# A decoder trunk on one core: the SBUF addresses of the split weights and of the differences of x are changed

## The chip, the core and the metric

The kernel runs on one core of a Trainium2 chip. The core has a matrix engine (TensorE, PE in the profile, with its weight loads shown apart as PEld), VectorE (DVE), ScalarE (ACT), GpSimd (POOL) and SyncE (SP), which issues transfers. The engines work on SBUF, a memory of 128 partitions; a tile has the same byte address in each of them, and "address" means that byte within a partition here. TensorE multiplies a stationary operand of 128 x 128 (loaded by LDWEIGHTS) with an operand that is streamed past it, and writes to PSUM.

The metric is the device time in microseconds. The kernel before takes 1767.03 us (median of 2 runs, 1766.98 to 1767.09).

## The reference

Two post-norm decoder layers on 512 tokens of width 1024, float32. Each layer is a SwiGLU feed-forward, a mixer and a second feed-forward, each followed by a LayerNorm.

```python
def swiglu_ffn(x, w_gu, w_down):
    a, u = jnp.split(x @ w_gu, 2, axis=-1)
    return (jax.nn.silu(a) * u) @ w_down

for l in range(DEPTH):
    x = layer_norm(DEEPNORM_ALPHA * x + 0.5 * swiglu_ffn(x, ffn1_w_gu[l], ffn1_w_down[l]),
                   ln1_g[l], ln1_b[l])
    x = layer_norm(DEEPNORM_ALPHA * x + hybrid_mixer(x, w_in[l], w_out[l], attn_sinks[l],
                                                     rope_cos, rope_sin, ret_cos, ret_sin),
                   ln2_g[l], ln2_b[l])
    x = layer_norm(DEEPNORM_ALPHA * x + 0.5 * swiglu_ffn(x, ffn2_w_gu[l], ffn2_w_down[l]),
                   ln3_g[l], ln3_b[l])
```

The hidden width of a feed-forward is 2816. The mixer projects x to attention and retention heads, computes both, and projects the result back.

## The kernel before

**Split products.** Every large product is made of three matmuls (`mm3`, L183 to L185). A float32 operand is split into a high part, rounded to the type fp32r by ScalarE (`split`, L168), and a low part, the rest, made by VectorE (L169). The three matmuls are high x high, high x low, low x high. In the rows of the profile L183, L184 and L185 follow each other, over and over.

**Units.** Weights come from HBM into one of two raw tiles (`raw`, `rawp`), and are split in pieces of 128 x 1024 elements, called units: a high tile `uh` and a low tile `ul`. The pool `unit` holds six of each (`UBUFS`), taken in turn; `Weights.pump` splits the next unit as soon as one of the six is given back. Everything that reads a unit after that is TensorE. In the gate and up projections and the mixer's projections by columns a unit is the stationary operand and x is streamed; in the down product and in the projections by tokens the unit is streamed, 512 columns at a time, and x or the hidden state is stationary.

**x and its differences.** x lies transposed in `xh` and `xl` (its high and low parts, 16,384 bytes each). For nine of the eleven column pairs of a feed-forward, gate and up are computed by a scheme of seven products instead of eight on blocks of half the contraction and half the tokens (`glu7`). Three products stream blocks of x itself, and four stream differences of its blocks, which `sums_of_x` writes once per feed-forward into the tiles `Th` and `Tl` (16,384 bytes each, four blocks). All these matmuls have 256 columns. The down product uses the same scheme on blocks of 256 x 512 x 10 chunks, with `xh` and `xl` as the room for the split hidden state, and 512 columns.

**Order.** Each engine runs its instructions in program order, which the code writes out by hand: products in sequence, splits of the next units between them.

**Addresses.** The pools are laid out in SBUF in the order in which they are made, each tile behind the one before: `base` (identity, `mhalf`, `xh`, `xl`, `Y`), `rawp`, `unit` (first the six `uh`, then the six `ul`), `small`, and then the pools of each stage, which take turns in the rest. Tiles of 4096 bytes follow each other without gaps, so all six `uh` have the same address modulo 256, and so have the chunks within a tile, whose steps are 512, 1024 and 2048 bytes. In the built program the starts are, modulo 256:

```
identity 128   mhalf 128   xh 160   xl 160   Y 160   raw 160
uh 160 (all six)   ul 160 (all six)
hT, S, R, Th, Tl, hr, tail units 96        mixer's q, k, pT, yah, yal, vr 32
```

Of the kernel before, what the change touches and what calls it, by code (L numbers as in the profile page):

```python
# [7 lines left out]
F32 = mybir.dt.float32  # L8
F32R = mybir.dt.float32r
# [9 lines left out]
P = 128  # L19
# [27 lines left out]
class Weights:  # L47


    def __init__(self, T, items):  # L50
        self.T, self.items = T, items
        self.emitted = self.taken = self.out = 0
        self.ready = []
        self.raws = {}
        self.last = {raw: i for i, (raw, _, _, _) in enumerate(items)}
# [44 lines left out]
class Trunk:  # L100
    def __init__(self, tc, ctx):
        self.tc, self.nc = tc, tc.nc
        self.n = 0
        self.now = 0
        self.pin = True
        self.tasks = []
        self.later = []
        self.pace = None
        self.halves = 2
        nc = self.nc  # L110
        self.base = ctx.enter_context(tc.tile_pool(name="base", bufs=1))
        self.rawp = ctx.enter_context(tc.tile_pool(name="rawp", bufs=2))
        self.unit = ctx.enter_context(tc.tile_pool(name="unit", bufs=UBUFS))
        self.small = ctx.enter_context(tc.tile_pool(name="small", bufs=3))
        self.psum = ctx.enter_context(tc.tile_pool(name="psum", bufs=8, space=PSUM))
        self.ident = self.base.tile([P, P], F32, name="ident")
        make_identity(nc, self.ident)
        self.mhalf = self.base.tile([P, 8], F32, name="mhalf")
        nc.vector.memset(self.mhalf, -0.5)
        self.xh = self.base.tile([P, KC, SEQ], F32R, name="xh")  # L120
        self.xl = self.base.tile([P, KC, SEQ], F32R, name="xl")
        self.Y = self.base.tile([P, NT, D], F32, name="Y")
# [37 lines left out]
    def units(self, pool=None, tag="u", bufs=None):  # L160
        pool = pool or self.unit
        kw = {} if bufs is None else {"bufs": bufs}
        hi = pool.tile([P, 1024], F32R, tag=tag + "h", name=self.nm("uh"), **kw)
        lo = pool.tile([P, 1024], F32R, tag=tag + "l", name=self.nm("ul"), **kw)
        return hi, lo

# [356 lines left out]
    def ffn(self, g_, b, out=None):  # L523
        nc, tc, W = self.nc, self.tc, self.W
        with ExitStack() as ctx:
# [3 lines left out]
            gp = self.gpool = gctx.enter_context(tc.tile_pool(name=self.nm("ffng"), bufs=1))  # L529
            hT = hpool.tile([P, NF, SEQ], F32, name=self.nm("hT"))  # L530
            H = KC // 2
            Th = gp.tile([P, 4, H, 256], F32R, name=self.nm("Th"))
            Tl = gp.tile([P, 4, H, 256], F32R, name=self.nm("Tl"))

            def sums_of_x():

# [136 lines left out]
            pool = self.fpool = ctx.enter_context(tc.tile_pool(name=self.nm("ffnd"), bufs=1))  # L673
# [80 lines left out]
            def take():  # L754
                u, h = W.get(), ahead.pop(0)
                ahead.append(next(split, None))
                return u, h
# [17 lines left out]
            for n, (banks, new, more) in enumerate((  # L775
# [12 lines left out]
                for g in range(GROUPS):  # L788
                    u, h = take()
# [398 lines left out]
```

## Time and profile before

| | |
|---|---|
| median of the runs | 1767.03 us |
| span of the profiled execution | 1765.1 us |
| instructions | 29166 |
| HBM read | 212.38 MB, 122 GB/s over the span |

The profiled execution is one run on the chip; its span is 1.9 us shorter than the median of the runs. Its page gives busy times by engine, a strip of 40 slices, and the chain of work that ended last: from the last instruction back to whatever released each step. Groups of instructions carry a count, a busy sum and a mean duration. For matmuls the duration includes the way through the array, during which the next one runs already, so it is not the interval at which they start; intervals are read from start times in the order of time. A weight load (PEld) runs beside the matmul before it.

### The profile page before, as it was taken

Reading aid. Unit: us, or ns where it says so; the run is one execution under the profiler, and the core shown is the slowest. Engines: PE = TensorE matmul, PEld = TensorE weight load, DVE = VectorE, ACT = ScalarE, POOL = GpSimd, SP = SyncE. Lnnn points to the kernel's source line nnn. Section 1 sums busy time; section 2 is a strip of 40 time slices with the busy share of each in tenths; the row PEclk is TensorE's granted clock in tenths of the full one; section 3 lists DMA queues with packets and bytes.
Section 4 is the critical chain, followed back from the end, with each engine's and each line's share of the span. In section 5 each row is a group of like instructions: output and inputs, shape, how many; then the busy total and the mean of one; then the engine's idle time right before and its main releaser. Section 6 shows DMA issues by size and latency. Waiting matters only on the chain.

```text
span 1765.1 us, 29166 instructions
## 1 busy us (share of the span) xinstructions
PE 1752.7 (99%) x11930; PEld 1600.5 (91%) x11930; DVE 1414.9 (80%) x1975; ACT 928.1 (53%) x1456; POOL 182.9 (10%) x152
## 2 busy tenths in 40 slices
PE   9999999999999999999999999999999999999998
PEld 9999988887789999998899999889877899999886
DVE  7888888856767888878888888888567587888887
ACT  5455556378712455555535555554795234555561
POOL 0000022111111000014000000311011110000131
PEclk9999999999999999999999999999999999999999
DMA  6234389422222243369423334982233122334891
GB/s 191 97 96 133 131 202 199 131 85 88 73 79 72 74 137 102 97 208 214 140 68 99 121 96 147 211 203 91 85 95 96 48 95 97 97 96 132 211 218 48
DMA packets 163765, 216.34 MB, mean 123 GB/s; under 512 B 5168, under 2 KB 116528, under 8 KB 163632
## 3 DMA queue, kind: packets, MB, share of 16 engines
q1 hardware_dynamic: 141872, 172.55, 30.5%
q0 software_dynamic: 21760, 41.95, 13.1%
q8 instruction: 93, 1.52, 0.3%
q14 instruction: 40, 0.33, 0.1%
HBM read 212.38 MB, written 2.10 MB: 122 GB/s over the span
## 4 chain that ended last, share of the span: by engine, by line
PE 90%; issue 6%; DMA 1%; DVE 1%; POOL 1%; ACT 0%; SPq 0%; POOLq 0%; DVEq 0%
PE ps L183 29%; PE ps L185 29%; PE ps L184 29%; PE ps L476 1%; DMA raw<-in_ffn_w_gu_dram 1%; POOL sw L959 1%; PE ps L1067 1%; PE ps L1015 0%; PE ps L1029 0%; PE ps L1063 0%; PE ps L1050 0%; DMA retS<-c_retS_dram 0%; ACT sw L957 0%; DVE ul L169 0%; PE ps L1007 0%
## 5 line engine op out<-in xcount | busy, mean ns | idle before, releaser
L183 PE MATMUL ps<-xh,uh 128*128 128x256 f32 (+1 forms) x1616 | 482.2, 298 | 0.0
L185 PE MATMUL ps<-xh,ul 128*128 128x256 f32 (+1 forms) x1616 | 479.3, 297 | 1.0 <-DVE ul L169 0.9
L184 PE MATMUL ps<-xl,uh 128*128 128x256 f32 (+1 forms) x1616 | 478.5, 296 | 0.3 <-DVE xl L169 0.3
L168 ACT CAST uh<-raw 128x1024 fp32r<-128x1024 f32 (+1 forms) x274 | 237.1, 886 | 245.6 <-PE ps L184 140.1
L169 DVE TENSOR_TENSOR ul<-raw,uh 128x1024 fp32r<-128x1024 f32 (+1 forms) x274 | 273.3, 1013 | 62.2 <-ACT uh L168 61.6
L183 PE MATMUL ps<-Th,uh 128*128 128x256 f32 x1152 | 319.1, 277 | 0.0
L184 PE MATMUL ps<-Tl,uh 128*128 128x256 f32 x1152 | 318.7, 277 | 0.0
L185 PE MATMUL ps<-Th,ul 128*128 128x256 f32 x1152 | 318.3, 276 | 0.0
L185 PEld LDWEIGHTS ps<-xh,ul 128*128 128x128 f32 x1616 | 307.9, 191 | 10.1 <-DVE ul L169 1.6
L183 PEld LDWEIGHTS ps<-xh,uh 128*128 128x128 f32 x1616 | 307.9, 191 | 9.7 <-issue 1.6
L184 PEld LDWEIGHTS ps<-xl,uh 128*128 128x128 f32 x1616 | 308.0, 191 | 7.9 <-DVE xl L169 0.5
L183 PE MATMUL ps<-uh,xh 128*128 128x512 f32 x720 | 283.4, 394 | 0.5 <-ACT xh L168 0.5
L185 PE MATMUL ps<-uh,xl 128*128 128x512 f32 x720 | 280.8, 390 | 0.0
L184 PE MATMUL ps<-ul,xh 128*128 128x512 f32 x720 | 280.3, 389 | 0.0
L168 ACT CAST uh<-S 128x1024 fp32r<-128x1024 f32 x144 | 151.1, 1049 | 149.0 <-PE ps L184 145.2
L169 DVE TENSOR_TENSOR ul<-S,uh 128x1024 fp32r<-128x1024 f32 x144 | 175.9, 1222 | 60.1 <-ACT uh L168 59.5
L184 PEld LDWEIGHTS ps<-Tl,uh 128*128 128x128 f32 x1152 | 216.7, 188 | 0.0
L183 PEld LDWEIGHTS ps<-Th,uh 128*128 128x128 f32 x1152 | 216.6, 188 | 0.0
L185 PEld LDWEIGHTS ps<-Th,ul 128*128 128x128 f32 x1152 | 216.4, 188 | 0.0
L389 POOL DMA_DIRECT2D R<-in_ffn_w_down_dram x80 | 97.1, 1217 | 1020.7 <-DVE ul L169 930.0
L169 DVE TENSOR_TENSOR ul<-R,uh 128x1024 fp32r<-128x1024 f32 x120 | 145.1, 1221 | 25.8 <-ACT uh L168 25.7
L183 PEld LDWEIGHTS ps<-uh,xh 128*128 128x128 f32 x720 | 135.2, 188 | 30.1 <-issue 1.6
(143 smaller groups left out, 2362.4 us busy)
## 6 DMA issues: line engine op xcount, KB each, us to landing
raw<-in_ffn_w_gu_dram SPq DMA_DIRECT2D x86, 1024.0 KB, 5.5
R<-in_ffn_w_down_dram POOLq DMA_DIRECT2D x80, 512.0 KB, 7.6
raw<-in_w_in_dram SPq DMA_DIRECT2D x18, 1024.0 KB, 5.2
R<-in_ffn_w_down_dram SPq DMA_DIRECT2D x16, 1024.0 KB, 6.3
raw<-in_ffn_w_down_dram SPq DMA_DIRECT2D x12, 1024.0 KB, 7.2
R<-in_ffn_w_down_dram SPq DMA_DIRECT2D x8, 512.0 KB, 4.3
raw<-in_w_in_dram SPq DMA_DIRECT2D x8, 512.0 KB, 6.1
raw<-in_w_out_dram SPq DMA_DIRECT2D x8, 512.0 KB, 6.4
```

Of the source, the lines that this page charges most:

```text
L168: a = self.nc.scalar.copy(hi, src)
L169: b = self.low = self.nc.vector.tensor_sub(lo, src, hi.bitcast(F32))
L183: keep(mm(out, ah, bh, start=start, stop=False, **kw))
L184: keep(mm(out, ah, bl, start=False, stop=False, **kw))
L185: keep(mm(out, al, bh, start=False, stop=stop, **kw))
L389: self.nc.gpsimd.dma_start(src, rows(i, j, g * 2, 2), accum_op=ALU.add))
L476: nc.tensor.transpose(b[:, c * P : (c + 1) * P], src[:, c * P : (c + 1) * P], self.ident)
L959: nc.gpsimd.tensor_mul(sw[:, :n], sw[:, :n], S)
L1067: ins = nc.tensor.matmul(ob[:, o0 : o0 + HD], ST[h][:, n, :], vr[:, n, p * P + h * HD : p * P + (h + 1) * HD], start=n == 0, stop=n == 0 o ...
```

## The change

No computation changes, and no instruction, transfer or wait is added, removed or moved: on each of the five engines the same instructions stand in the same order before and after. Tiles get other addresses.

- The high tiles of the pool `unit` get 1032 elements instead of 1024, of which the first 1024 are used, so each starts 32 bytes further on, modulo 256, than the one before.
- `mhalf` moves from the pool `base` to a pool `near` of its own between `rawp` and `unit`. What followed it in `base` starts 32 bytes earlier; `unit` starts where it did.
- `Th` and `Tl` get 8 elements more, and their contents start 4 elements (16 bytes) in, in the first feed-forward of each layer, and at 0 in the second.
- The rest of SBUF follows: what lies behind the units moves by 192 bytes.

```diff
+        self.near = ctx.enter_context(tc.tile_pool(name="near", bufs=1))
+        self.mhalf = self.near.tile([P, 8], F32, name="mhalf")
+        nc.vector.memset(self.mhalf, -0.5)
         self.unit = ctx.enter_context(tc.tile_pool(name="unit", bufs=UBUFS))
...
-        self.mhalf = self.base.tile([P, 8], F32, name="mhalf")
-        nc.vector.memset(self.mhalf, -0.5)
...
-        hi = pool.tile([P, 1024], F32R, tag=tag + "h", name=self.nm("uh"), **kw)
+        width = 1032 if pool is self.unit else 1024
+        hi = pool.tile([P, width], F32R, tag=tag + "h", name=self.nm("uh"), **kw)[:, :1024]
         lo = pool.tile([P, 1024], F32R, tag=tag + "l", name=self.nm("ul"), **kw)
...
-            Th = gp.tile([P, 4, H, 256], F32R, name=self.nm("Th"))
-            Tl = gp.tile([P, 4, H, 256], F32R, name=self.nm("Tl"))
+            self.ffns += 4
+            off = self.ffns % 8
+            Th, Tl = (gp.tile([P, 4 * H * 256 + 8], F32R, name=self.nm(n))[:, off : off + 4 * H * 256]
+                      .rearrange("p (i k t) -> p i k t", i=4, k=H) for n in ("Th", "Tl"))
```

The starts in the built program after the change, modulo 256:

```
identity 128   xh 128   xl 128   Y 128   raw 128   mhalf 128
uh 160, 192, 224, 0, 32, 64   ul 96 (all six)
Th 48, Tl 80 (first feed-forward of a layer)    Th 32, Tl 64 (second)
hT, S, R, hr, tail units 32        mixer's q, k, pT, yah, yal, vr 224
```

More of the change, by code (lines that the diff above doesn't have):

```diff
@@ L109, in __init__ @@
         self.halves = 2
+        self.ffns = 0
         nc = self.nc
```

## The prediction

> **What bounds the kernel now.** I read the page first: busy shares, the clock row and the chain that ended last.
>
> ```profile
> span 1765.1 us, 29166 instructions
> ...
> PE 1752.7 (99%) x11930; PEld 1600.5 (91%) x11930; DVE 1414.9 (80%) x1975; ACT 928.1 (53%) x1456; POOL 182.9 (10%) x152
> ...
> PEclk9999999999999999999999999999999999999999
> ...
> PE 90%; issue 6%; DMA 1%; DVE 1%; POOL 1%; ACT 0%; SPq 0%; POOLq 0%; DVEq 0%
> PE ps L183 29%; PE ps L185 29%; PE ps L184 29%; PE ps L476 1%; DMA raw<-in_ffn_w_gu_dram 1%; POOL sw L959 1%; PE ps L1067 1%; PE ps L1015 0%; PE ps L1029 0%; PE ps L1063 0%; PE ps L1050 0%; DMA retS<-c_retS_dram 0%; ACT sw L957 0%; DVE ul L169 0%; PE ps L1007 0%
> ```
>
> TensorE is busy for 99% of the span at a full granted clock, and the three lines of `mm3` are 87% of the chain. Next the waits of TensorE, all of them:
>
> ```profile
> PE ps L468 <- POOL ident masks.py:199: 1.4, 1, 1.4
> PE ps L185 <- DVE ul L169: 0.9, 2, 0.7
> PE ps L1029 <- DVE rr L1032: 0.8, 2, 0.4
> PE ps L183 <- ACT xh L168: 0.5, 2, 0.2
> PE ps L476 <- DMA Y<-in_x_dram: 0.3, 1, 0.3
> PE ps L184 <- DVE xl L169: 0.3, 1, 0.3
> ```
>
> They add up to 4.2 us of 1765.1. So the time is the number of matmuls times the interval at which TensorE starts them. Third, the groups of its lines by form; the counts are what I need from them (the means are modelled durations that overlap, not intervals):
>
> ```profile
> L183 PE MATMUL ps<-xh,uh 128*128 128x256 f32 x1408 | 398.5, 283 | 0.0
> ...
> L183 PE MATMUL ps<-Th,uh 128*128 128x256 f32 x1152 | 319.1, 277 | 0.0
> ...
> L183 PE MATMUL ps<-uh,xh 128*128 128x512 f32 x720 | 283.4, 394 | 0.5 <-ACT xh L168 0.5
> ...
> L183 PE MATMUL ps<-xh,uh 128*128 128x512 f32 x208 | 83.6, 402 | 0.0
> ...
> L183 PE MATMUL ps<-b,yah 128*128 128x512 f32 x64 | 25.3, 396 | 0.0
> L183 PE MATMUL ps<-uh,hr 128*128 128x512 f32 x64 | 25.2, 394 | 0.0
> ...
> L183 PE MATMUL ps<-uh,uh 128*128 128x512 f32 x32 | 12.5, 389 | 0.0
> ```
>
> Each has a twin of equal count at L184 and L185, so 256-column matmuls that stream x: 3 x 1408 = 4224; 256-column ones that stream a difference of x: 3 x 1152 = 3456; 512-column ones with a unit from the pool of six: 3 x (720 + 208 + 32) = 2880; 512-column ones without such a unit: 3 x 128 = 384.
>
> Last the intervals, from the order of time inside a feed-forward. Start times are in us, rounded to 10 ns, so I count over many rows:
>
> ```profile
> 74.16 0.29 PE L183 MATMUL ps<-Th,uh 128*128 128x256 f32 x1
> ...
> 74.52 0.28 PE L183 MATMUL ps<-Th,uh 128*128 128x256 f32 x1
> 74.63 0.28 PE L184 MATMUL ps<-Tl,uh 128*128 128x256 f32 x1
> ...
> 76.78 0.28 PE L185 MATMUL ps<-Th,ul 128*128 128x256 f32 x1
> 76.90 0.28 PE L183 MATMUL ps<-xh,uh 128*128 128x256 f32 x1
> ...
> 78.08 0.28 PE L184 MATMUL ps<-xl,uh 128*128 128x256 f32 x1
> ...
> 79.52 0.28 PE L184 MATMUL ps<-xl,uh 128*128 128x256 f32 x1
> ```
>
> From 74.63 to 76.78 are 19 intervals: 113.2 ns each, streaming a difference. From 78.08 to 79.52 are 12: 120.0 ns each, streaming x. Same shape, same weights' pool, same clock, 6.8 ns apart. The switch is not sharp: the first ten after 76.90 take 1.18 us (118 ns), the first three after 74.16 take 0.36 us (120 ns). Beside them stands what runs at the same time:
>
> ```profile
> 78.32 0.28 PE L183 MATMUL ps<-xh,uh 128*128 128x256 f32 x1
> 78.32 0.19 PEld L184 LDWEIGHTS ps<-xl,uh 128*128 128x128 f32 x1
> ```
>
> The load of the next matmul's weights starts with the stream of this one. Both read SBUF. In the program before, x starts at byte 160 modulo 256, every unit at 160, a difference at 96. I call distance the start of the next weights minus the start of the streamed operand, modulo 256: it is 0 in the 120 ns rows and 64 in the 113 ns rows, with chunk steps of 512, 1024 and 2048 bytes that don't alter it. This is the only reading by which the change can matter.
>
> The same for 512 columns, in the down product:
>
> ```profile
> 305.83 0.39 PE L183 MATMUL ps<-uh,xh 128*128 128x512 f32 x1
> ...
> 307.87 0.39 PE L183 MATMUL ps<-uh,xh 128*128 128x512 f32 x1
> ...
> 319.90 0.39 PE L185 MATMUL ps<-uh,hr 128*128 128x512 f32 x1
> ...
> 322.43 0.39 PE L184 MATMUL ps<-ul,xh 128*128 128x512 f32 x1
> ```
>
> Nine intervals in 2.04 us are 226.7 ns, at distance 0. The eleven from 319.90 take 2.53 us, 230.0 ns: there the streamed unit changes from a tail unit at 96 to a pool unit at 160, so one distance is 64 and the next ones are 0 again, and it costs time until the two streams are in step again.
>
> **The change, part by part.** No instruction, transfer or wait is added, removed or moved; the five engines' orders are the same. Only addresses differ, so every term is a count times a shift of an interval.
>
> *Moved constants, outputs, staging.* x and the raw weights go from 160 to 128, mhalf and the small tiles elsewhere, the tiles behind the units by up to 192 bytes. Those of ScalarE, VectorE and the queues I take at 0; what hides a change of theirs is that TensorE waits 4.2 us in all, that VectorE is idle for 20% and ScalarE for 47% of the span. If that cover went, the splits of L169 at 80% of VectorE would be late first.
>
> *x against the units* (4224 matmuls). Distances become 32, 64, 96, 128, 160 or 192 by buffer where the next weights are a high part (two matmuls of three), and 224 where they are a low part. Never 0. Bounds: 0 if they stay at 120.0, -6.7 ns if all run as the differences do (113.3, from 113.2 and the repeating 0.11, 0.11, 0.12 of the rows). The rows just after a switch lie between, at 118. One of seven new distances, 64, is known; the others I put in the middle, 116.7: -3.3 x 4224 = -14.1 us. Ends: -28.3 and 0.
>
> *Differences against the units* (3456). From 64 everywhere they go to 112, 144, 176, 208, 240 or 16 for high parts in the first feed-forward of a layer and 128, 160, 192, 224, 0 or 32 in the second (there a buffer meets distance 0, which costs 120 in the rows above); 16 or 32 for low parts. They leave the cheaper of the two known distances, so they can hardly gain. Middle again: +3.3 x 3456 = +11.5 us. Ends 0 and +6.7 x 3456 = +23.2. The 16-byte shift goes into this term; alone it has no row, and it touches half of these matmuls, so its bounds are the term's halves.
>
> *512 columns* (2880). Distances go from 0 to 64, 96, 128, 160, 192 or 224 with a streamed high part, 32 with a streamed low part, and those of x against units in the projections. The load of the next weights takes as long (0.19 us) as beside 256 columns, so I let the overlap cost the same: half of 6.7 saved, -3.3 x 2880 = -9.6 us. Ends: -6.7 x 2880 = -19.3, and +3.3 x 2880 = +9.5, by the 230.0 rows. The 384 others keep distance 0 and their time.
>
> *Sum.* -14.1 + 11.5 - 9.6 = -12.2 us. The profiled execution is 1765.1 us, so 1752.9; the median of the runs lies 1.9 us above it, which I add: 1754.8, say 1755.
>
> **The rivals.**
>
> *Nothing happens, 1767.* 120 against 113 ns may come from the tiles' form: x is read as 256 tokens out of rows of 512, the differences as contiguous blocks. The change leaves these forms, so all terms are 0 and the time is 1767. Against it: both are read in runs of 1 KB, and the interval drifts over ten matmuls after a switch, which a form would not do. The page of the Trainium skill "SBUF — State Buffer", section "Who interferes with whom", speaks for this rival: it gives TensorE two independent read ports, one for the streamed operand and one for the weights, and says "PE and ACT never wait on anyone". By that rule no distance could matter, and the trace agrees with it only if the 6.8 ns have this other cause. Chance 0.15.
>
> *Zero is the one bad distance.* Then x gains 28.3, 512 columns 19.3, and the differences lose only where distance 0 appears, on one buffer of six in half the feed-forwards: two thirds of 3456 / 12 = 192 matmuls at 6.7 ns, 1.3 us. Sum -46.3: 1721. For it: the only two distances measured. Against: the 230.0 rows, where a single distance of 64 made things worse for ten matmuls, and in the changed kernel the distance changes at every third matmul. Chance 0.17, spread from 1720 to 1742.
>
> *The differences lose more than the rest gains, 1786.* Place: the seven products of `glu7`. Price: they leave the good distance for mixed ones and go to 120, +23.2; x, mixed too, stays near 119 (-4.2) and 512 columns stay. Sum +19: 1786. It decides for slower as soon as the differences rise by more than 1.22 times what x falls (4224 / 3456), the 512-column term at 0. For it: the slow first matmuls after each switch; a triple now meets two or three distances, so no steady step may form. With 512 columns at 230 as well it is 1795. Chance 0.25.
>
> **How the numbers follow.** My case, between 1743 and 1768, has 0.43; the rivals 0.15, 0.17, 0.25. Two per cent, about what a measurement of this kernel can tell from no change, is 35.3 us: below 1731.7 or above 1802.4. Of the second rival some two thirds lie below 1731.7: faster 0.11. The third reaches from 1768 to some 1805, and a tenth of it lies above 1802.4: slower 0.03. The rest, 0.86, is within. The range leaves out about 0.11 below and 0.09 above, so it goes from 1733 to 1788.
>
> **What would show it.** In the order of time of the changed kernel: 256-column matmuls on x at 113 to 118 ns instead of 120 (first term), those on differences at 115 to 119 instead of 113 (second), 512-column ones at 220 to 226 instead of 227 (third). Intervals that differ between the six buffers would show that distance is the variable; equal ones, 120 and 113 as before, the first rival. I am wrong as a whole if x stays at 120 while differences rise, or if waits on ACT or VectorE appear in front of L183 to L185.

## The result, and the profile after

| | before | after |
|---|---|---|
| median of the runs | 1767.03 us | 1788.69 us |
| ratio to before, 95% interval | | 1.0122 [1.0106, 1.0139] |
| span of the profiled execution | 1765.1 us | 1786.4 us |
| TensorE busy | 1752.7 us | 1775.5 us |

The changed kernel is slower by 1.2%. First its page, the same lines as before:

```profile
span 1786.4 us, 29166 instructions
...
PE 1775.5 (99%) x11930; PEld 1610.2 (90%) x11930; DVE 1417.2 (79%) x1975; ACT 928.2 (52%) x1456; POOL 181.8 (10%) x152
...
PEclk9999999999999999999999999999999999999999
...
PE 98%; DMA 1%; DVE 1%; ACT 0%; SPq 0%; POOLq 0%; issue 0%; DVEq 0%
```

The instruction counts and the clock are the same, VectorE and ScalarE are busy about as long as before (1414.9 and 928.1 us then), and TensorE is busy 22.8 us longer. Its waits are no longer than before, 2.6 us in all instead of 4.2:

```profile
PE ps L471 <- POOL ident masks.py:199: 1.4, 1, 1.4
PE ps L186 <- ACT xh L171: 0.5, 2, 0.2
PE ps L187 <- DVE xl L172: 0.3, 1, 0.3
PE ps L479 <- DMA Y<-in_x_dram: 0.2, 1, 0.2
PE ps L188 <- DVE ul L172: 0.2, 1, 0.2
```

So the loss is in the intervals between matmuls. The order of time in the same feed-forward shows them (start in us, duration, engine, line; L186 to L188 are `mm3` here):

```profile
73.75 0.28 PE L186 MATMUL ps<-Th,uh 128*128 128x256 f32 x1
...
76.45 0.28 PE L188 MATMUL ps<-Th,ul 128*128 128x256 f32 x1
76.57 0.28 PE L186 MATMUL ps<-xh,uh 128*128 128x256 f32 x1
...
80.58 0.28 PE L187 MATMUL ps<-xl,uh 128*128 128x256 f32 x1
```

Differences: 23 intervals in 2.70 us, 117.4 ns instead of 113.2. x: 34 in 4.01 us, 117.9 instead of 120.0. The sharp contrast between the two is gone. And the down product:

```profile
304.64 0.39 PE L186 MATMUL ps<-uh,xh 128*128 128x512 f32 x1
...
309.47 0.39 PE L186 MATMUL ps<-uh,xh 128*128 128x512 f32 x1
```

21 intervals in 4.83 us: 230.0 ns instead of 226.7. The groups by form answer to those shown before (count | busy, mean ns; the means were 283, 277 and 394):

```profile
L186 PE MATMUL ps<-xh,uh 128*128 128x256 f32 x1408 | 396.3, 281 | 0.0
...
L186 PE MATMUL ps<-Th,uh 128*128 128x256 f32 x1152 | 323.2, 281 | 0.0
...
L186 PE MATMUL ps<-uh,xh 128*128 128x512 f32 x720 | 286.3, 398 | 0.5 <-ACT xh L171 0.5
```

These means are no intervals, but they move with them: x got quicker by 2 ns, differences and 512 columns slower by 4. Over the whole trace of each kernel I took the start-to-start time of every pair of these matmuls that follow each other without a break (under 300 ns):

| kind of matmul | count | before, ns | after, ns | sum, us |
|---|---|---|---|---|
| 256 columns, x | 4211 | 119.8 | 118.7 | -4.3 |
| 256 columns, differences | 3456 | 113.9 | 118.0 | +14.0 |
| 512 columns, a unit streamed past x or hidden state | 2095 | 227.1 | 232.1 | +10.4 |
| 512 columns, x streamed past a unit | 568 | 228.2 | 231.7 | +2.0 |
| 512 columns, the rest | 468 | 227.7 | 228.9 | +0.5 |

The sum is +22.6 us, against +21.3 us of span, in which the waits are 1.6 us shorter. The time is found; the question is why nearly everything went to about 118 and 232 ns.

### The profile page after: what moved, and what is told of

The parts are those of the page before. It is cut to its first block, busy times and chain, and to the rows that moved or that the text cites. A ratio compares the mean times of both kernels' runs of the same rounds, so it can differ in the third digit from the quotient of the medians.

```text
span 1786.4 us, 29166 instructions
## 1 busy us (share of the span) xinstructions
PE 1775.5 (99%) x11930; PEld 1610.2 (90%) x11930; DVE 1417.2 (79%) x1975; ACT 928.2 (52%) x1456; POOL 181.8 (10%) x152
## 4 chain that ended last, share of the span: by engine, by line
PE 98%; DMA 1%; DVE 1%; ACT 0%; SPq 0%; POOLq 0%; issue 0%; DVEq 0%
PE ps L186 31%; PE ps L187 31%; PE ps L188 31%; PE ps L479 1%; DMA raw<-in_ffn_w_gu_dram 1%; PE ps L1020 1%; PE ps L985 1%; PE ps L1072 1%; PE ps L1012 1%; PE ps L1034 1%; PE ps L1068 0%; PE ps L1055 0%; PE ps L1045 0%; DVE ul L172 0%; ACT uh L171 0%; DVE xl L172 0%
## 5 line engine op out<-in xcount | busy, mean ns | idle before, releaser
L186 PE MATMUL ps<-xh,uh 128*128 128x256 f32 (+1 forms) x1616 | 480.7, 297 | 0.0
L188 PE MATMUL ps<-xh,ul 128*128 128x256 f32 (+1 forms) x1616 | 477.3, 295 | 0.3 <-DVE ul L172 0.2
L187 PE MATMUL ps<-xl,uh 128*128 128x256 f32 (+1 forms) x1616 | 476.8, 295 | 0.3 <-DVE xl L172 0.3
L188 PE MATMUL ps<-Th,ul 128*128 128x256 f32 x1152 | 323.2, 281 | 0.0
L186 PE MATMUL ps<-Th,uh 128*128 128x256 f32 x1152 | 323.2, 281 | 0.0
L187 PE MATMUL ps<-Tl,uh 128*128 128x256 f32 x1152 | 323.1, 281 | 0.0
L188 PEld LDWEIGHTS ps<-xh,ul 128*128 128x128 f32 x1616 | 303.9, 188 | 10.2 <-DVE ul L172 0.7
L186 PEld LDWEIGHTS ps<-xh,uh 128*128 128x128 f32 x1616 | 303.7, 188 | 10.2 <-issue 1.6
L187 PEld LDWEIGHTS ps<-xl,uh 128*128 128x128 f32 x1616 | 303.9, 188 | 8.6 <-DVE xl L172 0.5
L186 PE MATMUL ps<-uh,xh 128*128 128x512 f32 x720 | 286.3, 398 | 0.5 <-ACT xh L171 0.5
L187 PE MATMUL ps<-ul,xh 128*128 128x512 f32 x720 | 284.3, 395 | 0.0
L188 PE MATMUL ps<-uh,xl 128*128 128x512 f32 x720 | 283.8, 394 | 0.0
L187 PEld LDWEIGHTS ps<-Tl,uh 128*128 128x128 f32 x1152 | 217.0, 188 | 0.0
L186 PEld LDWEIGHTS ps<-Th,uh 128*128 128x128 f32 x1152 | 216.9, 188 | 0.0
L188 PEld LDWEIGHTS ps<-Th,ul 128*128 128x128 f32 x1152 | 216.7, 188 | 0.0
L186 PEld LDWEIGHTS ps<-uh,xh 128*128 128x128 f32 x720 | 135.4, 188 | 33.8 <-issue 1.6
```

The lines of the kernel that those rows point to most:

```text
L186: keep(mm(out, ah, bh, start=start, stop=False, **kw))
L187: keep(mm(out, ah, bl, start=False, stop=False, **kw))
L188: keep(mm(out, al, bh, start=False, stop=stop, **kw))
```

## The experiments

All start from the kernel before. "Distance" is again the start of the weights that are loaded next minus the start of the streamed operand, modulo 256; three theories were put against each other: price (each distance has its price), in-step (a constant distance lets the two streams settle, a mixture doesn't), form (the tiles' form and not the distance makes 120 or 113).

### The three parts, one at a time

The step of the six high tiles alone:

```diff
-        hi = pool.tile([P, 1024], F32R, tag=tag + "h", name=self.nm("uh"), **kw)
+        width = 1032 if pool is self.unit else 1024
+        hi = pool.tile([P, width], F32R, tag=tag + "h", name=self.nm("uh"), **kw)[:, :1024]
```

> Only the step of 32 bytes between the six high tiles; mhalf and the differences' tiles as before. Distances of x become 0, 32, 64, 96, 128 or 160 by buffer and 192 to low parts. In-step theory (the interval depends on whether the distance stays the same from matmul to matmul; mixed distances keep the two streams of TensorE from settling): this part alone carries the loss, differences near 118 ns, x near 118, 512 columns near 232, +15 to +25 us, ratio 1.009 to 1.014. Price theory (every distance has a price of its own and a mixture costs the mean): x meets distance 0 again and pays 120 there, so x is no cheaper than before or in the changed kernel; +15 to +30 us, but the intervals sort by buffer, with buffer 1 at 120 and buffer 3 at 113. Form theory (120 against 113 comes from the tiles' form): no change, ratio 1.000.

Measured: 1784.05 us, ratio 1.0098 [1.0081, 1.0115]. Differences 118.3 ns, x 117.6, unit streamed with 512 columns 231.1. This part alone costs 17.1 us, where all three cost 21.7; the in-step and the price theory both gave this size. The form theory is out, since what TensorE reads has the same form as before. The built program says which of the six buffers each matmul reads. By buffer, x sorts in part as the price theory said: at the buffer with distance 64 the matmuls before a high part take 114.9 and 115.4 ns, those of the five other buffers 116.5 to 119.8. The differences, none of whose high parts meets 64 here, lie between 116.6 and 119.5 whatever the buffer.

`mhalf` alone, so that x lies 32 bytes ahead of all units:

```diff
+        self.near = ctx.enter_context(tc.tile_pool(name="near", bufs=1))
+        self.mhalf = self.near.tile([P, 8], F32, name="mhalf")
+        nc.vector.memset(self.mhalf, -0.5)
...
-        self.mhalf = self.base.tile([P, 8], F32, name="mhalf")
-        nc.vector.memset(self.mhalf, -0.5)
```

> Only mhalf moved, so x starts at 128 and every unit at 160: one distance, 32, for all matmuls that stream x, and 224 for the 512-column ones that stream a unit; differences keep 64. In-step theory: one repeating interval for each kind, at a settled value such as 113.3 or 120 for x and 220 or 226.7 for 512 columns, differences 113.3: the time is between 2.7% faster and the same. Price theory, with the prices that the changed kernel shows as means (119 for x, 232 for 512 columns): x -4 us, 512 columns +14 us, ratio 1.003 to 1.008. Form theory: 1.000.

Measured: 1781.79 us, ratio 1.0084 [1.0069, 1.0099]. The distance is constant within each kind, and yet nothing settles at a cheap step: x streams at 118.6 ns, in a cycle of 116 to 122, and the unit with 512 columns at 233.3 ns. So the in-step theory is wrong in its plain form, that any constant distance will do. The price theory's 1.003 to 1.008 came nearest and is just missed: it let the differences keep their time, but at their unchanged distance of 64 they rose from 113.9 to 115.4 ns (+4.9 us), with some 2000 intervals at 113 to 115 ns and 1400 at 116 to 120. The groups by form (count | busy, mean ns) show the 512-column term, whose mean was 394 before:

```profile
L184 PE MATMUL ps<-uh,xh 128*128 128x512 f32 x720 | 287.2, 399 | 0.5 <-ACT xh L169 0.5
```

The tiles of the differences alone:

```diff
+        self.ffns = 0
...
-            Th = gp.tile([P, 4, H, 256], F32R, name=self.nm("Th"))
-            Tl = gp.tile([P, 4, H, 256], F32R, name=self.nm("Tl"))
+            self.ffns += 4
+            off = self.ffns % 8
+            Th, Tl = (gp.tile([P, 4 * H * 256 + 8], F32R, name=self.nm(n))[:, off : off + 4 * H * 256]
+                      .rearrange("p (i k t) -> p i k t", i=4, k=H) for n in ("Th", "Tl"))
```

> Only the tiles of the differences changed (8 elements more each, and 16 bytes of shift in every second feed-forward); x and units as before at distance 0. Distances of the differences become 48 to high and 16 to low parts in the first feed-forward of a layer, 64 and 32 in the second, so two distances in every triple. In-step theory: the differences go from 113.3 to 116 to 118 ns in both kinds of feed-forward, +9 to +16 us, ratio 1.005 to 1.009; x and 512 columns unchanged. Price theory: 64 keeps 113.3, so the second feed-forward loses at most a third of its matmuls' price, +0 to +8 us. Form theory: 1.000.

Measured: 1784.31 us, ratio 1.0098 [1.0083, 1.0113]. Only the differences move much, from 113.9 to 118.8 ns or +16.9 us, just over the in-step theory's 16. The groups by form have x at 283 and 512 columns at 394 as before, and the differences at 282 instead of 277:

```profile
L184 PE MATMUL ps<-Th,uh 128*128 128x256 f32 x1152 | 325.0, 282 | 0.0
```

In the second feed-forward of a layer, where no contents are shifted and only `Tl` starts 32 bytes further on, the three matmuls of `mm3` meet 64, 32 and 64 and take 119.3, 122.3 and 115.3 ns. At the same 64 all three took 113.2 to 114.3 in the kernel before. So a matmul doesn't have the price of its own distance when its neighbours have others: this speaks against the plain price theory.

Each part alone costs 15 to 17 us, all three 21.7: they don't add up.

### The distances of x and differences exchanged

```diff
+        self.near = ctx.enter_context(tc.tile_pool(name="near", bufs=1))
+        self.gap = self.near.tile([P, 16], F32, name="gap")
...
+            gp.tile([P, 16], F32, name=self.nm("gap"))
             Th = gp.tile([P, 4, H, 256], F32R, name=self.nm("Th"))
```

> 64 bytes are left free behind the raw tiles and 64 ahead of the differences: x then has distance 64 and the differences distance 0, the reverse of before; 512 columns that stream a unit have 192. Form theory: nothing changes, 120 on x and 113.3 on differences, ratio 1.000. Both distance theories: x 113.3 (-28 us), differences 120 (+23 us). For 512 columns the in-step theory expects one repeating interval, 220 or 226.7 (-19 or 0 us), so in all -24 to -5 us, ratio 0.986 to 0.997; the price theory with 232 at 192 expects +14 us there, in all +9, ratio 1.005.

Measured: 1773.35 us, ratio 1.0038 [1.0023, 1.0053]. x 115.3 ns, most often 113; differences 119.4, most often 120; unit with 512 columns 229.0, x with 512 columns 233.2. The groups by form, x at 283 and differences at 277 ns before:

```profile
L185 PE MATMUL ps<-xh,uh 128*128 128x256 f32 x1408 | 392.6, 279 | 0.4 <-ACT uh L170 0.4
L185 PE MATMUL ps<-Th,uh 128*128 128x256 f32 x1152 | 325.3, 282 | 0.0
```

The two have changed places without any change of form, so the distance makes the contrast between them. The total lies between the two expectations since 512 columns at 192 cost 229, a middle price.

### More distances

Gaps of 96, 128 and 192 bytes behind the raw tiles, and other gaps ahead of the differences, in the same places as above.

> 96 bytes free behind the raw tiles and 160 ahead of the differences: x at distance 96, differences at 160, streamed units against x at 160, everything constant within its kind. Price theory: a repeating cycle for each kind, 256 columns somewhere between 113 and 120 ns, 512 columns 227 to 234, and the means of the changed kernel (119 for x, 118 for differences, 232 for 512 columns) come out as the means of these prices. In-step theory in its first form (any constant distance settles at 113.3 or 120, 220 or 226.7) is already contradicted by the 116 to 122 ns at distance 32; if it has anything, 512 columns are at 226.7 here.

> 128 bytes free behind the raw tiles and 96 ahead of the differences: x at distance 128, streamed units against x at 128, differences at 224. Price theory: x and differences between 113 and 120 ns; 512 columns at 230 to 236, since a lone 128 cost some 10 ns over two matmuls in the kernel before. In-step theory: 226.7 for 512 columns, since nothing changes from matmul to matmul.

> 192 bytes free behind the raw tiles and 224 ahead of the differences: x at distance 192, differences at 96, streamed units at 64 against x. Price theory: differences at 96 cost what x cost at 96 (118.5 ns), which the form of the tile would have to change; 512 columns at 64 cost what x streamed with 512 columns cost there (233.2 ns); x at 192 was not seen yet, 116 to 120. Form theory: differences stay cheaper than x.

Measured, one execution each: 1797.37, 1785.77 and 1785.37 us. With the earlier runs, mean intervals in ns (x and differences where both were seen):

| distance | 256 columns | 512 columns, unit streamed | 512 columns, x streamed |
|---|---|---|---|
| 0 | 119.8, 119.4 | 227.1 | 228.2 |
| 32 | 118.6 | not seen | 233.2 |
| 64 | 114.6, 113.3 | 233.4 | 233.3 |
| 96 | 118.6, 117.3 | not seen | 234.0 |
| 128 | 118.9 | 232.4 | 232.8 |
| 160 | 119.8 | 233.4 | not seen |
| 192 | 118.1 | 229.0 | 229.3 |
| 224 | 116.8 | 233.3 | not seen |

With 256 columns 64 is the one good place; with 512 columns 0 is, 192 is second, and everything else lies at 232 to 234. The e_x96 run was the slowest of all, as every kind sits at a bad distance there. Differences and x at the same distance lie at most 1.3 ns apart (117.3 and 118.6 at 96); at 64 that gap is not one of form, as the last experiment shows. Counting modulo 256 fits. In the row of 192, x starts 64 bytes before the streamed unit (modulo 512 as well), but the unit starts 192 bytes after the streamed x, and the intervals are 229.0 and 229.3 ns; the row of 64 has the same two ways to count, with 233.4 and 233.3.

### All addresses moved together

```diff
+        self.gap = self.base.tile([P, 8], F32, name="gap")
         self.ident = self.base.tile([P, P], F32, name="ident")
```

> 32 bytes free ahead of the identity: every tile starts 32 bytes further on, so x and units now start at a multiple of 64, and all distances are those of before. Distance theories: 120, 113.3 and 226.7 as before, ratio 0.998 to 1.002. Alignment theory (what the changed kernel altered is where x starts within a line of 64 bytes): x loses or gains, 113 or 118 ns instead of 120, ratio off by 0.5% or more.

Measured: 1766.85 us, ratio 1.0002 [0.9993, 1.0011], intervals 119.8, 113.9 and 227.1 as before. So a shift of all tiles by 32 bytes is of no weight; the differences between starts are what counts.

### Two distances mixed

64 free bytes between the six high and the six low tiles, so each triple meets 0 and 64 on x, 0 and 192 when units are streamed; 192 bytes ahead of the differences keep them at 64 to the high parts.

> The six low tiles lie 64 bytes further on than the high ones (modulo 256), x and high tiles level: within each triple the distance is 0 to high and 64 to low weights for x, 64 and 128 for differences. If the weights being loaded are what the stream meets, L184 (whose successor loads a low part) is the fast one of x, 113 to 116 ns, and L183 and L185 stay near 120; if it is the weights in use, L185 (which uses a low part) is the fast one. If a mixture blurs the prices, as the means by buffer in the changed kernel do, all three lie between 116 and 120. Differences rise from 113.9 to 115 to 118 in each case.

Measured, one execution: 1787.21 us. x at 118.2 ns: the mean of two 119.8 and one 113.3 would be 117.6. But the streamed unit at 231.9, above both of the distances that it meets (227.1 and 229.0), and differences at 118.2, where two 113.3 and one 118.9 have the mean 115.2. The order of time in the down product:

```profile
299.78 0.39 PE L186 MATMUL ps<-uh,xh 128*128 128x512 f32 x1
...
303.94 0.40 PE L186 MATMUL ps<-uh,xh 128*128 128x512 f32 x1
```

18 intervals in 4.16 us, 231 ns. So a mixture of cheap distances isn't cheap here. In each run with such a mixture the high and the low tiles of one operand also lie at different addresses modulo 256 from each other, and no run tells the two apart. Of the three lines on x, L187, during which a low part is loaded, is at 117.6 ns and the two others at 118.4 and 118.5: too close to tell whether the weights in use or the weights being loaded are met. That stays open.

### Cheap distances, kept constant

Two views of one tile, 64 bytes apart: x of the feed-forwards in the first, x of the mixer and the hidden state of the down product in the second. The views overlap, so 16 tokens at the edge of some blocks are overwritten through the other view: the same instructions on other values, and the result is no longer that of the reference.

```diff
+        X = self.base.tile([P, 2 * KC * SEQ + 16], F32R, name="xh")
+        self.far, self.level = ([X[:, o + j * KC * SEQ : o + (j + 1) * KC * SEQ].rearrange("p (k t) -> p k t", k=KC)
+                                 for j in range(2)] for o in (0, 16))
+        self.xh, self.xl = self.far
...
```

> x lies 64 bytes ahead of the units' address in the feed-forwards and level with it in the mixer; the hidden state of the down product lies level with it too (one tile, two views 64 bytes apart); differences at 64 as before. So 256 columns meet 64 in the feed-forwards, 512 columns 0. Price theory: x in the feed-forwards goes from 119.8 to 113.4 ns without slow first matmuls at the switches between x and differences, differences from 113.9 to 113.4, 512 columns unchanged at 227: -24 to -27 us, ratio 0.985 to 0.987. If overlapping views add waits between stages, 0.990.

Measured: 1746.84 us, ratio 0.9889 [0.9872, 0.9905]. x 114.8 ns (113.9 to 114.3 in the feed-forwards, 120.6 in the mixers, where its distance is 0), differences 113.3 with none of the slow matmuls at the switches, unit with 512 columns 227.2. The gain of 19.9 us falls short of the 24 to 27 expected, since x is not at 113.4 throughout.

The simple version, which computes the whole reference, has one gap of 64 bytes behind the raw tiles, as in the exchanged kernel but with nothing ahead of the differences:

> 64 bytes free behind the raw tiles and nothing else: x and differences both at distance 64 to the units, streamed units at 192 against x. Price theory, from the prices of the runs before (113.4 ns for 256 columns at 64, 229.0 for 512 columns at 192, 233.2 for x streamed with 512 columns at 64): 4210 x -6.4 ns = -27 us at most, differences -2 us since the switches cost nothing any more, 2095 x +1.9 = +4 us, 568 x +5 = +3 us: -18 to -22 us, ratio 0.987 to 0.990. If other engines' addresses matter, less.

Measured: 1750.81 us, ratio 0.9903 [0.9887, 0.9920]. From its groups by form:

```profile
L185 PE MATMUL ps<-xh,uh 128*128 128x256 f32 x1408 | 391.2, 278 | 1.5 <-ACT uh L170 1.5
```

x 114.6 ns, differences 113.3, streamed unit 229.1, x with 512 columns 233.3: -21.9, -2.0, +4.0 and +2.9 us, -17.0 in sum, and 16.1 measured, against 18 to 22 expected: 114.6 instead of 113.4 on x is the difference. It is faster than both kernels: one tile of 64 unused bytes.

That 114.6 is a mean of two levels, though x has the distance 64 everywhere in this kernel. In the pairs with seven products x takes 113.3 ns, as the differences do, so the form of the tile makes no difference there. In the projections of the mixers it takes 118.1 and 118.5. One stretch of each, the mixer's first:

```profile
353.11 0.28 PE L185 MATMUL ps<-xh,uh 128*128 128x256 f32 x1
...
356.29 0.28 PE L185 MATMUL ps<-xh,uh 128*128 128x256 f32 x1
...
620.04 0.28 PE L185 MATMUL ps<-xh,uh 128*128 128x256 f32 x1
...
621.40 0.28 PE L185 MATMUL ps<-xh,uh 128*128 128x256 f32 x1
```

27 intervals in 3.18 us are 117.8 ns, 12 in 1.36 us are 113.3. Nothing but mm3 runs on TensorE between the rows of either stretch. So at 64 a sequence of equal matmuls can run at either of two steps and can keep the dear one; the differences did the same in the run with `mhalf` alone. The code is not what decides: the first pairs of the second feed-forward run the same `proj` as the mixer, and there 210 of 286 intervals are at 113 or 114 ns and 41 at 117 or 118. What does decide was not tested.

## Why the prediction was wrong

**What bounds the kernel, and that distance is the variable.** Right. The exchanged kernel shows it as directly as can be, and the kernel with all addresses moved by 32 bytes shows that a shift which leaves the distances alone changes nothing. Distance is not all: the neighbours' distances count too, and at one distance two steps were seen. The first rival, that nothing happens, is out, and the measurement decides against the rule of the page of the Trainium skill "SBUF — State Buffer", section "Who interferes with whom", as far as it says that PE waits for nobody: by the distance between the streamed operand and the weights a 256-column matmul costs up to 6.5 ns more here, and a 512-column one up to 6. The other engines and the transfers are not needed for it. Where no instruction of VectorE, ScalarE or GpSimd and no DMA packet overlaps an interval of the streamed unit, that interval is 227.1 ns in the kernel before (115 intervals) and 232.0 in the changed one (119).

**The moved constants, outputs and staging, at nothing.** Right: the other engines are busy as long as before, and the waits did not grow.

**x against the units, -14.1 us.** Right in sign, too large: -4.3. (This product and the next two were worked with half of 6.7, 3.35, or a value next to it, though 3.3 is printed; that changes them by 0.2 us.) The middle of 113.3 and 120 was no fair guess for an unknown distance, since the unknown ones lie near the upper end: 116.8 to 119.8 in the table. Of the signs named beforehand, x at 113 to 118 was just missed with 118.7. The six buffers do differ, as the prediction asked: in front of a high part x takes 117.0 and 117.7 ns at the buffer at 64 and 117.2 to 121.8 at the others. But the two matmuls at one buffer differ as well, by up to 4.6 ns (121.8 and 117.2 at 128), so the distance alone doesn't set them.

**Differences against the units, +11.5 us.** Right: +14.0, or 118.0 ns, within the named 115 to 119. They left the cheap distance, as was said; that the three distances of a triple also disturb each other was the third rival's reason.

**512 columns, -9.6 us.** This is the step that failed: it measured +12.9 (10.4 + 2.0 + 0.5). "The load of the next weights takes as long (0.19 us) as beside 256 columns, so I let the overlap cost the same" carried the sign of the 256-column matmuls over to the 512-column ones. The table shows that their prices have another order: with 512 columns distance 0 is the cheapest of all, and the kernel before stood on it. So no new distance could bring the 220 to 226 ns that the prediction named as the sign; they came out at 232. The rows of the kernel before had shown a price at 0 only, and the 230.0 ns after a lone 64 were read as an end of the range where they were the best evidence of the sign.

**The rivals.** The third, "the differences lose more than the rest gains", came nearest: 1786 against 1788.7, with its mechanism of triples that meet two or three distances. Its parts were +23.2 from the differences and -4.2 from x; the time came as 14.0 from the differences, -4.3 from x and 12.9 from 512 columns, of which it had none but in its last sentence. The second, zero as the one bad distance, fell at distance 32 already, where x takes 118.6. The range ended at 1788, 0.7 us below the result.

What stands behind all of it, as far as the runs go: there are a few distances at which a sequence of equal matmuls can run in a cheap steady step (113.3 ns at 64 with 256 columns, 227 at 0 with 512, to a lesser degree 229 at 192), and a common level of 117 to 120 and 231 to 234 ns for nearly everything else, other constant distances and most mixtures of cheap ones alike (224 with 256 columns, 116.8, and the triples at 64, 192 and 64 in the run with the step alone, 115 where a high part follows, lie between). At 64 a sequence can stay at that level too. Before, differences and 512 columns stood on cheap steps by the accident of pool sizes, and only x didn't. The change took both off and brought x to the common level from just above it. That is also why the three parts don't add up: each one alone takes some matmuls to that level, and they can't be taken there twice. The differences lose 14.9, 4.9 and 16.9 us in the runs with one part each, in the order above, and 14.0 with all three; the 512-column matmuls with x lose 10.8, 15.6, 0.0 and 12.5. How the two operands' reads meet inside the chip, and so why these distances, was not measured.

## What to carry to other kernels

When an engine is busy for 99% and a kernel's matmuls of one shape start at two different intervals, compare the addresses of what they read. Make the distance between streamed operand and weights the same for all matmuls in a row, then scan it in steps of 32 bytes by one unused tile, for each column count by itself. Then read the intervals stage by stage, since a good distance alone didn't bring the cheap step everywhere here. A layout that gives each buffer of a ring its own offset mixes distances, and here a mixture of good ones was mostly no longer good.

## What the runs showed of the hardware that was not expected

- The best distance depends on the number of streamed columns: 64 for 256 columns (113.3 ns) and 0 for 512 (227.1 ns); each is at the dear end for the other (119.8 ns at 0, 233.4 at 64).
- One distance can have two steps: at 64, 256 columns ran at 113.3 ns in the feed-forwards and at 117.8 in a stretch of the mixer of the same kernel.
- A sequence that alternates between two fairly cheap distances is dearer than either: 231.9 ns where 0 alone takes 227.1 and 192 alone 229.0.
- A few bytes between two tiles are worth 17 us of 1767 (the differences' tiles alone). In every second feed-forward of that run only `Tl` moves, by 32 bytes, and the differences go from 113.9 to 119.0 ns.
